# A gated delta-rule block on one core: ScalarE's copies of the turned inverse are queued behind the evictions that are counted off ahead of the level steps

## The chip, the cores and the metric

The kernel runs on one core of a Trainium2 chip. The metric is the device time of one execution in microseconds (us). The core has five engines that each work through a queue of instructions in order: PE (TensorE, matmuls), DVE (VectorE), ACT (ScalarE), POOL (GpSimd) and SP (SyncE, which here only issues DMAs). In the rows of the profile PEld is the loading of weights on PE, and L924 is line 924 of the kernel's file.

## The reference

The program is one block of a network on a sequence of 1024 tokens of width 1024: a modulated norm, dilated attention of 8 heads beside a gated delta rule of 8 heads, an output projection, and a gated feed-forward layer. What matters here is the delta rule, which works in chunks; the kernel solves the triangular system below with an explicit inverse.

```python
def _chunk_gated_delta_rule(q, k, v, g, beta):
    ...
    a_mat = jnp.where(strict, jnp.einsum('nbhcd,nbhed->nbhce', k_beta, kc) * decay, 0.0)
    rhs = jnp.concatenate([vc * bc[..., None], k_beta * jnp.exp(gcum)[..., None]], axis=-1)
    sol = lax.linalg.triangular_solve(a_mat + jnp.eye(CHUNK, dtype=a_mat.dtype), rhs,
                                      left_side=True, lower=True, unit_diagonal=True)
    u, w = sol[..., :dv], sol[..., dv:]
    ...
    _, o = lax.scan(step, state0, (qc, kc, u, w, gcum, qk))

def reference(x, c, w_ada, ...):
        ...
        proj = h @ w_in[l]
        q_a, k_a, v_a, q_d, k_d, v_d, z_d, b_d, a_d = jnp.split(proj, split_points, axis=-1)
        y_attn = _dilated_attention(q_a.reshape(hs), k_a.reshape(hs), v_a.reshape(hs), rel_bias).astype(x.dtype)
        y_delta = _gated_deltanet(q_d, k_d, v_d, z_d, b_d, a_d, conv_w[l], a_log[l], dt_bias[l], delta_norm_g[l])
        y = jnp.concatenate([y_attn, y_delta], axis=-1) @ w_out[l]
        x = x + g1 * y
        ...
```

## The kernel before

**Stages.** The eight delta heads are worked in two groups of four, `delta(0)` and `delta(1)`. Each group convolves and turns its q and k, prepares the decayed products, inverts a triangular matrix per chunk of 128 tokens, and then scans the chunks. Attention, the output projection and the feed-forward layer follow. All products in full precision are split into a high and a low part and take three matmuls each (high by high, high by low, low by high).

**Projections as filler.** The other projections of the input (`others()`: z0, kd, qd, vd, z1, va0, a4_0, a0_0, va1 and so on) are a Python generator that yields after each step with an estimate of its time. The group's code draws steps from it: `ahead(us)` draws so many microseconds, `turn(name)` draws the amount that the table `FILL` has for a product and queues that product on PE behind the last matmul drawn, and `hold(what, us)` draws until a projection is done and then so many microseconds more. A projection of kind `proj_d` (kd, qd, vd, a4, a0) makes two halves of 512 tokens, eight steps of three matmuls each (L590); one of kind `proj_t` (z, va) makes eight row blocks, eight steps of three matmuls each (L613). After a half or a block its eviction is traced, when the generator is asked for the next step: two copies of 128x256 in `spill` (L1096), one in `va_evac` (L1087) or an activation in `z_evac`. The evictions run on ScalarE under `urgent()`, which puts them early in the scheduler's preference. Sums lie in two PSUM banks ("g"), and the evicted copies in four SBUF buffers (tag "ev", bufs=4), each of which is written out to DRAM by a DMA on SP's queue (L1097, L1088).

**Order.** Each engine's queue is written ahead of the run by a scheduler that goes by priorities and by its own estimate of when an instruction's inputs are ready. `tc.issue_after(ins)` adds an order on the engine of `ins`: what is traced in its block is queued behind `ins`, without a wait for its end.

**The inverse.** `delta_inverse(g, st)` inverts 32x32 blocks on VectorE (the loop of L886 and L890 fills `tt`), writes `tt` to DRAM (L893) and loads it back in another layout as `tn` (L895). Then come the level steps, per head a generator `head(hl_)`: its first part does the product `lv` (L918) on PE from `tn`, clears `U` and a part of `t64`, turns the blocks of `tn` into `U` on VectorE (L923) and copies two blocks of `tn` into `t64`, the lower half of a tile `tc_` (L924 and L925, on ScalarE, 32x256 each). The second product fills `lv` again (L933, L937), ScalarE copies its results into `t64` and `U` (L939 to L941), and the products `lw` (L947, reads `t64`) and `lx` (L955) follow, with a copy into `U` (L957). The heads are started four steps apart (`SKEW`), but tiles `tc_` have three buffers, so three heads' copies can be done early. Ahead of the first head the kernel calls `hold(*LEVELS[g])`, which is ("qd", 4) in group 0 and ("z1", 46) in group 1, and takes `front`, the last matmul drawn; the first part of each head is queued behind it on PE. Nothing orders the ScalarE copies of that first part.

Of the kernel before, what the change touches and what calls it, by code (L numbers as in the profile page):

```python
# [12 lines left out]
AF = mybir.ActivationFunctionType  # L13
# [69 lines left out]
def build(tc, I, out):  # L83
    nc = tc.nc
# [20 lines left out]
    def urgent():  # L105
        return tc.high_priority(offset=6000)
# [40 lines left out]
    def gbank(name):  # L147
        return psb(name, "g", 2)
# [4 lines left out]
    def tbank(name):  # L153
        return psb(name, "t", 2)
# [36 lines left out]
    for j in range(3):  # L191
        n = min(HALF, 1152 - HALF * j)
        ps = tbank(f"ps_R{j}")
# [242 lines left out]
    for i in range(2):  # L436
        ps = aux[:, P * i : P * i + P]
# [119 lines left out]
        nc.scalar.activation(dst, dst, AF.Silu)  # L557

    kd, qd = {}, {}
    last = [None]  # L560
    fill = [None]
    used = [0.0]

# [11 lines left out]
    @contextmanager  # L575
    def turn(name):

        with tc.issue_after(last[0].ins) if ahead(FILL.get(name, 0)) else ExitStack():
            yield
# [43 lines left out]
    for q in range(2):  # L623
        ps = gbank(f"g_qd{q}")
# [5 lines left out]
    def z_evac(g):  # L630
        def f(tb, ps):
            zt = pv.tile([P, 256], F32, name=f"zt{g}_{tb}", tag="ev", bufs=4)
            with urgent():
                nc.scalar.activation(zt, ps[:, 0:256], AF.Silu)
            nc.gpsimd.tensor_tensor(
                out=zt.rearrange("p (h d) -> p h d", h=4),
                in0=zt.rearrange("p (h d) -> p h d", h=4),
                in1=ngh.unsqueeze(1).to_broadcast([P, 4, 64]), op=ALU.mult,
            )
            nc.sync.dma_start(_.zg[TB * g + tb], zt)  # L640
        return f
# [56 lines left out]
    def bc(v, n):  # L698
        return v.unsqueeze(len(v.shape)).to_broadcast(list(v.shape) + [n])
# [167 lines left out]
    def delta_inverse(g, st):  # L867

        nt = pr.tile([P, 32, 32], F32, name=f"nt{g}", tag="dt", bufs=2)
        nc.sync.dma_start(nt.rearrange("p j i -> p (j i)"), _.lt[g])  # L870
        bpr = pd.tile([P, 32], F32, name=f"bpr{g}", tag="nbpT", bufs=1)
        nc.sync.dma_start(
            bpr, bass.AP(tensor=_.bp[g].tensor, offset=_.bp[g][0:1, :].offset, ap=[[32, P], [1, 32]])
        )
        nc.vector.tensor_tensor(
            out=nt, in0=nt, in1=bpr.unsqueeze(1).to_broadcast([P, 32, 32]), op=ALU.mult
        )
        tt = pr.tile([P, 32, 32], F32, name=f"tt{g}", tag="dt", bufs=2)
        ttf = tt.rearrange("p i c -> p (i c)")
        nc.gpsimd.memset(ttf, 0.0)  # L880
        nc.gpsimd.memset(ttf[:, 0:1024:33], 1.0)
        for j in range(31):
            m = 31 - j
            tmp = pd.tile([P, 256], F32, name=f"tm{g}_{j}", tag="tm", bufs=1)
            tv = tmp[:, 0 : m * (j + 1)].rearrange("p (i c) -> p i c", i=m)
            nc.vector.tensor_tensor(  # L886
                out=tv, in0=bc(nt[:, j, j + 1 : 32], j + 1),
                in1=tt[:, j, 0 : j + 1].unsqueeze(1).to_broadcast([P, m, j + 1]), op=ALU.mult,
            )
            nc.vector.tensor_tensor(  # L890
                out=tt[:, j + 1 : 32, 0 : j + 1], in0=tt[:, j + 1 : 32, 0 : j + 1], in1=tv, op=ALU.add
            )
        nc.sync.dma_start(_.tn[g], ttf)  # L893
        tn = pr.tile([P, 32, 32], F32, name=f"tn{g}", tag="dt", bufs=2)
        nc.sync.dma_start(  # L895
            tn,
            bass.AP(tensor=_.tn[g].tensor, offset=_.tn[g][0:1, :].offset, ap=[[32, P], [4096, 32], [1, 32]]),
        )
        st["U"] = []

        def head(hl_):

            lt = st["lts"][hl_]
            nb = st["nbp"][:, :, hl_]
            tnh = tn[:, hl_ : 32 : 4, :]
            U = pd.tile([P, 8, P], F32, name=f"U{g}_{hl_}", tag="lu", bufs=5)
            st["U"].append(U)
            tc_ = pd.tile([P, 8, 64], F32, name=f"tc_{g}_{hl_}", tag="tc", bufs=TCB)
            t64, c2 = tc_[0:64], tc_[64:128]
            cs = pd.tile([P, 8, 32], F32, name=f"cs{g}_{hl_}", tag="cs", bufs=2)  # L910
            ps = tbank(f"lv{g}_{hl_}")
            pv = ps.rearrange("p (a n c) -> p a n c", a=2, n=8)
            with turn(f"la{g}_{hl_}"):
                for n in range(8):
                    for b in (0, 2):
                        lo = slice(32 * b, 32 * b + 32)
                        up = slice(32 * b + 32, 32 * b + 64)
                        nc.tensor.matmul(pv[up, 0, n, :], lt[lo, n, up], tnh[lo, n, :], start=True, stop=True)  # L918
            nc.gpsimd.memset(U, 0.0)
            nc.gpsimd.memset(t64[0:32, :, 32:64], 0.0)  # L920
            for b in range(4):
                bs = slice(32 * b, 32 * b + 32)
                nc.vector.transpose(U[bs, :, bs], tnh[bs])  # L923
            nc.scalar.copy(t64[0:32, :, 0:32], tnh[0:32])  # L924
            nc.scalar.copy(t64[32:64, :, 32:64], tnh[32:64])  # L925
            yield
            for b in (0, 2):
                up = slice(32 * b + 32, 32 * b + 64)
                nc.vector.tensor_tensor(out=cs[up], in0=pv[up, 0], in1=bc(nb[up], 32), op=ALU.mult)
            yield  # L930
            with turn(f"lb{g}_{hl_}"):
                for n in range(8):
                    nc.tensor.matmul(pv[32:64, 1, n, :], U[32:64, n, 32:64], cs[32:64, n, :], start=True, stop=True)  # L933
                    for b in (0, 2):
                        lo = slice(32 * b, 32 * b + 32)
                        up = slice(32 * b + 32, 32 * b + 64)
                        nc.tensor.matmul(pv[lo, 1, n, :], cs[up, n, :], U[up, n, up], start=True, stop=True)  # L937
            yield
            nc.scalar.copy(t64[32:64, :, 0:32], pv[32:64, 1])  # L939
            nc.scalar.copy(U[0:32, :, 32:64], pv[0:32, 1])  # L940
            nc.scalar.copy(U[64:96, :, 96:128], pv[64:96, 1])  # L941
            yield
            ps = sbank(f"lw{g}_{hl_}")
            pw = ps.rearrange("p (n c) -> p n c", n=8)
            with turn(f"lc{g}_{hl_}"):
                for n in range(8):
                    nc.tensor.matmul(pw[64:128, n, :], lt[0:64, n, 64:128], t64[:, n, :], start=True, stop=True)  # L947
            yield
            nc.vector.tensor_tensor(out=c2, in0=pw[64:128], in1=bc(nb[64:128], 64), op=ALU.mult)
            yield  # L950
            ps = tbank(f"lx{g}_{hl_}")
            px_ = ps.rearrange("p (n c) -> p n c", n=8)
            with turn(f"ld{g}_{hl_}"):
                for n in range(8):
                    nc.tensor.matmul(px_[0:64, n, :], c2[:, n, :], U[64:128, n, 64:128], start=True, stop=True)  # L955
            yield
            nc.scalar.copy(U[0:64, :, 64:128], px_[0:64])  # L957

        heads = []
        for step in range(3 * SKEW + 8):  # L960
            for h in heads:
                next(h, None)
            if step % SKEW == 0 and step // SKEW < 4:
                if step == 0:
                    hold(*LEVELS[g])
                    front, quiet[0] = last[0].ins, True
                heads.append(head(step // SKEW))
                with tc.issue_after(front):
                    next(heads[-1])
        quiet[0] = False  # L970
# [112 lines left out]
    def va_evac(c):  # L1083
        def f(tb, ps):
            t = pv.tile([P, 256], F32, name=f"va{c}_{tb}", tag="ev", bufs=4)
            with urgent():
                nc.scalar.copy(t, ps[:, 0:256])  # L1087
            nc.sync.dma_start(_.va[c][:, :, tb].rearrange("i p d -> p i d"), t.rearrange("p (i d) -> p i d", i=2))  # L1088
        return f

    def spill(name, dst):
        def f(hf, ps):
            for i in range(2):
                t = pv.tile([P, 256], F32, name=f"sp_{name}_{hf}_{i}", tag="ev", bufs=4)
                with urgent():
                    nc.scalar.copy(t, ps[:, 256 * i : 256 * i + 256])  # L1096
                nc.sync.dma_start(dst[:, HALF * hf + 256 * i : HALF * hf + 256 * i + 256], t)  # L1097
        return f

# [77 lines left out]
    quiet = [False]  # L1177
# [256 lines left out]
    ps = abank("g2t")  # L1434
# [82 lines left out]
    for hf in range(2):  # L1517
# [4 lines left out]
        for d in range(KT):  # L1522
            slabs = [(wsplit(I["wo"][d, 0], 512, f"wo{d}_0_{hf}"), 0)]
            t = x2[d, hf]
            nc.sync.dma_start(t, _.xp[2 * d + hf])
            ps = (gbank, sbank)[d % 2](f"wo{d}_0_{hf}")
# [204 lines left out]
    for k in range(4):  # L1731
# [3 lines left out]
        t = px.tile([P, HALF], F32, name=f"t2_{k}", tag="m", bufs=5)  # L1735
# [232 lines left out]
```

## Time and profile before

| | |
|---|---|
| time, median of 3 runs | 1410.61 us (1410.28 to 1413.69) |
| time of the profiled execution | 1409.24 us |
| its span in the profile | 1407.2 us |
| mean granted clock of TensorE | 0.993 |
| PE busy | 1347.5 us (96%) |
| ScalarE busy | 661.7 us (47%) |
| DVE busy | 875.2 us (62%) |
| tc copies from tn (L924, L925) | 16 in all, 404 ns each (median) |

The profile is of one execution, which took a little less than the median of the runs. A row of the timeline gives the start in us from the span's start, the duration, the engine, the line, the operation with its tiles and shapes, and in brackets the idle time ahead of it and what ended that. A row of waits gives who waited for whom, the total in us, the number of times and the longest. A row of the view by stages gives the busy time of each engine in a stretch of the span, with the number of instructions in brackets.

### The profile page before, as it was taken

What the parts mean: (1) busy time and instruction counts of PE and PEld (TensorE: products, weight loads), DVE (VectorE), ACT (ScalarE), POOL (GpSimd) and SP (SyncE); (2) the same over time, 40 slices, a digit from 0 to 9 for tenths busy, and PEclk for the clock granted to TensorE, in tenths of its full rate; (3) what the DMA queues carried; (4) which work ended last, traced back from release to release, by engine and by line L of the source; (5) the groups of instructions that cost most, each with busy time, mean ns of one, the idle gap of its engine ahead of it and who ended that gap; (6) DMA issues with size and microseconds to landing.
All of it is one profiled execution on the core that took longest, in us unless ns stands there. A gap on an engine that the chain in (4) does not pass through costs nothing.

```text
span 1407.2 us, 24465 instructions
## 1 busy us (share of the span) xinstructions
PE 1347.5 (96%) x8984; PEld 1109.5 (79%) x8984; DVE 875.2 (62%) x1669; ACT 661.7 (47%) x1287; POOL 285.8 (20%) x267
## 2 busy tenths in 40 slices
PE   8999999998989899999989999999999999999997
PEld 4778877888878677777877878888888888888885
DVE  3687484656815533666227986667585776474487
ACT  4497514356224355766147743333333333444456
POOL 2345412444303344453153000000000000000000
PEclk9999999999999999999999999999999999999999
DMA  8665575486352345621485345545363665765566
GB/s 307 224 194 167 153 214 164 134 255 186 109 143 65 125 138 145 195 97 61 160 247 175 130 158 171 173 148 174 131 206 105 213 211 185 253 224 194 195 225 232
DMA packets 169872, 245.68 MB, mean 175 GB/s; under 512 B 32566, under 2 KB 73831, under 8 KB 169752
## 3 DMA queue, kind: packets, MB, share of 16 engines
q1 hardware_dynamic: 169752, 244.12, 53.5%
q8 instruction: 71, 1.16, 0.3%
q14 instruction: 49, 0.40, 0.1%
HBM read 181.30 MB, written 67.48 MB: 177 GB/s over the span
## 4 chain that ended last, share of the span: by engine, by line
PE 58%; DVE 3%; DMA 2%; issue 1%; ACT 1%; POOL 0%; SPq 0%; DVEq 0%; ACTq 0%; POOLq 0%
PE wua L1590 8%; PE wga L1590 8%; PE X L1785 6%; PE wo L590 5%; PE wgc L1590 4%; PE wuc L1590 4%; PE Z L1785 4%; PE g_a L590 3%; PE y L1348 3%; PE wgb L1590 2%; PE Y L1785 2%; PE wub L1590 2%; PE tr L1331 2%; PE S L1307 1%; PE S L1308 1%
## 5 line engine op out<-in xcount | busy, mean ns | idle before, releaser
L1580 DVE TENSOR_TENSOR wl_db<-wr_db,wh_db 128x512 fp32r<-128x512 f32 x77 | 53.2, 691 | 76.2 <-ACT wh_db L1579 75.9
L1579 ACT CAST wh_db<-wr_db 128x512 fp32r<-128x512 f32 x77 | 47.9, 622 | 98.4 <-PE X L1785 41.3
L1311 DVE CUSTOM_DVE_ANT_0 X<-S,ng 128x512 f32<-128x512 f32 (+3 forms) x64 | 36.9, 586 | 56.2 <-PE S L1308 37.8
L1785 PE MATMUL X<-wl_db,wh_da 128*128 128x512 f32 x176 | 68.6, 390 | 0.2 <-DVE wl_db L1580 0.2
L1785 PE MATMUL X<-wh_db,wh_da 128*128 128x512 f32 x176 | 68.6, 390 | 0.0
L1785 PE MATMUL X<-wh_db,wl_da 128*128 128x512 f32 x176 | 68.5, 389 | 0.0
L1316 ACT ACTIVATE X<-X,sc 128x128 f32<-128x128 f32 (+7 forms) x64 | 49.4, 773 | 38.3 <-DVE sc L1311 34.8
L1318 POOL TENSOR_SCALAR X<-X,sc 128x128 f32<-128x128 f32 (+7 forms) x64 | 50.5, 792 | 75.9 <-DVE sc L1317 72.6
L1580 DVE TENSOR_TENSOR wl_da<-wr_da,wh_da 128x512 fp32r<-128x512 f32 x77 | 52.7, 685 | 1.2 <-ACT wh_da L1579 1.2
L590 PE MATMUL g_a<-hh,wh_a 128*128 128x512 f32 x128 | 52.8, 412 | 0.0
L590 PE MATMUL wo<-yh,wh_wo 128*128 128x512 f32 x128 | 51.3, 403 | 0.8 <-DVE xo L1399 0.8
L590 PE MATMUL wo<-yl,wh_wo 128*128 128x512 f32 x128 | 50.4, 393 | 1.1 <-DVE yl L1410 1.1
L590 PE MATMUL g_a<-hh,wl_a 128*128 128x512 f32 x128 | 51.2, 400 | 0.0
L590 PE MATMUL g_a<-hl,wh_a 128*128 128x512 f32 x128 | 51.1, 399 | 0.0
L590 PE MATMUL wo<-yh,wl_wo 128*128 128x512 f32 x128 | 51.0, 398 | 0.0
L1579 ACT CAST wh_da<-wr_da 128x512 fp32r<-128x512 f32 x77 | 47.3, 616 | 5.9 <-PE wua L1590 5.8
L1331 PE MATMUL tr<-ident,X 128*128 128x128 f32 x288 | 44.0, 277 | 3.6 <-DVE et L1334 2.0
L1579 ACT CAST wh_wg_s<-wg_s 128x512 fp32r<-128x512 f32 x33 | 20.6, 623 | 56.1 <-PE wuc L1590 23.8
L231 POOL TENSOR_TENSOR wl_wo<-wr_wo,wh_wo 128x512 fp32r<-128x512 f32 x24 | 32.9, 1374 | 61.6 <-ACT wh_wo L230 61.6
L613 PE MATMUL g_va<-wh_va,hh 128*128 128x256 f32 x128 | 38.6, 301 | 5.8 <-ACT sp_a L1096 5.8
L1331 PEld LDWEIGHTS tr<-ident,X 128*128 128x128 f32 x288 | 33.2, 140 | 13.3 <-issue 4.3
L1348 PE MATMUL y<-et,va 128*64 128x128 f32 x576 | 43.2, 280 | 0.3 <-DVE yl L1360 0.3
(544 smaller groups left out, 4304.3 us busy)
## 6 DMA issues: line engine op xcount, KB each, us to landing
wm<-in_wada SPq DMA_DIRECT2D x44, 512.0 KB, 6.2
wr_da<-ao_d SPq DMA_DIRECT2D x77, 256.0 KB, 3.0
wr_wu<-in_wu SPq DMA_DIRECT2D x50, 256.0 KB, 2.8
wr_wg<-in_wg SPq DMA_DIRECT2D x48, 256.0 KB, 2.8
ao_d<-a SPq DMA_DIRECT2D x44, 256.0 KB, 2.3
wr_wd<-in_wdn SPq DMA_DIRECT2D x44, 256.0 KB, 3.0
wr_db<-wt_d SPq DMA_DIRECT2D x44, 256.0 KB, 2.8
ao_d<-as SPq DMA_DIRECT2D x33, 256.0 KB, 2.0
```

The source lines that it names most:

```text
L231: (eng or nc.gpsimd).tensor_tensor(out=lo[:, :n], in0=raw[:, :n], in1=hi[:, :n].bitcast(F32), op=ALU.subtract)
L590: last[0] = nc.tensor.matmul(ps, a[:, w0], b[k0 + k4][:, cs], start=(i == 0), stop=(i == n - 1))
L613: last[0] = nc.tensor.matmul(ps[:, :n], a[k][:, ts_], b[:, w0], start=(i == 0), stop=(i == 23))
L1311: nc.vector.tensor_tensor_reduce(out=X[:, c0:c1], in0=ps[:, 0 : c1 - c0], in1=ng[:, u + c0 : u + c1], scale=1.0, scalar=(3e38 if m is None ...
L1316: nc.scalar.activation(X[:, 0:nk], X[:, 0:nk], AF.Exp, scale=-1.0, bias=m, accum_out=sc[:, 2:3])
L1318: nc.gpsimd.tensor_scalar(out=X[:, 0:nk], in0=X[:, 0:nk], scalar1=sc[:, 3:4], scalar2=0.0, op0=ALU.mult, op1=ALU.add)
L1331: nc.tensor.transpose(ps[:, (kb - c0) * P : (kb - c0 + 1) * P], X[:, kb * P : kb * P + P], ident)
L1348: nc.tensor.matmul(yps[64 * e : 64 * e + 64, yc], va[:, kb, 64 * e : 64 * e + 64], ets[e][:, kb, :], start=(kb == 0), stop=(kb == qb),)
L1579: nc.scalar.copy(hi, src)
L1580: (eng or nc.vector).tensor_tensor(out=lo, in0=src, in1=hi.bitcast(F32), op=ALU.subtract)
L1590: nc.tensor.matmul(ps, a[:, w0], b, start=(first and k == 0 and n_ == 0), stop=(k == 3 and n_ == 2), skip_group_check=True,)
L1785: nc.tensor.matmul(bank[b], a[:, ts_], w, start=(first and f == 0 and n_ == 0), stop=(f == NF - 1 and n_ == 2), skip_group_check=True,)
```

## The change

The evictions of the other projections are remembered as they are traced: `taken[0]` is the last one. At the first step of the level steps, after the hold, each group keeps that eviction as `evicted`, beside `front`. The two ScalarE copies from `tn` into `t64` of all four heads are then traced under `tc.issue_after(evicted.ins)`: they are queued on ScalarE behind that eviction, and so behind all that were traced ahead of it, since evictions follow one another. No instruction is added, removed or resized.

```diff
-    last = [None]
+    last, taken = [None], [None]
...
             zt = pv.tile([P, 256], F32, name=f"zt{g}_{tb}", tag="ev", bufs=4)
             with urgent():
-                nc.scalar.activation(zt, ps[:, 0:256], AF.Silu)
+                taken[0] = nc.scalar.activation(zt, ps[:, 0:256], AF.Silu)
...
-            nc.scalar.copy(t64[0:32, :, 0:32], tnh[0:32])
-            nc.scalar.copy(t64[32:64, :, 32:64], tnh[32:64])
+            with tc.issue_after(evicted.ins):
+                nc.scalar.copy(t64[0:32, :, 0:32], tnh[0:32])
+                nc.scalar.copy(t64[32:64, :, 32:64], tnh[32:64])
...
                 if step == 0:
                     hold(*LEVELS[g])
-                    front, quiet[0] = last[0].ins, True
+                    front, evicted, quiet[0] = last[0].ins, taken[0], True
...
             t = pv.tile([P, 256], F32, name=f"va{c}_{tb}", tag="ev", bufs=4)
             with urgent():
-                nc.scalar.copy(t, ps[:, 0:256])
+                taken[0] = nc.scalar.copy(t, ps[:, 0:256])
...
                 t = pv.tile([P, 256], F32, name=f"sp_{name}_{hf}_{i}", tag="ev", bufs=4)
                 with urgent():
-                    nc.scalar.copy(t, ps[:, 256 * i : 256 * i + 256])
+                    taken[0] = nc.scalar.copy(t, ps[:, 256 * i : 256 * i + 256])
```

## The prediction

> **What bounds the kernel now.** First the head of the page, to see which engine sets the time.
>
> ```profile
> span 1407.2 us, 24465 instructions
> PE 1347.5 (96%) x8984; PEld 1109.5 (79%) x8984; DVE 875.2 (62%) x1669; ACT 661.7 (47%) x1287; POOL 285.8 (20%) x267
> ```
>
> PE is busy 1347.5 of 1407.2 us: it is the bound, and only time in which PE stands still, or runs slowly, can be won. Next the waits, asked for around the two places where the touched copies (tc, L924 and L925) run, 200 to 222 us (group 0) and 381 to 398 us (group 1).
>
> ```profile
> PE g_vd L590 <- ACT sp_qd L1096: 0.7, 1, 0.7
> ...
> ACT tc L924 <- DMA tn<-tn_d: 8.8, 1, 8.8
> PE g_va L613 <- ACT sp_a L1096: 5.8, 1, 5.8
> ```
>
> In group 1 PE stands 5.8 us for an eviction by ScalarE (sp_a), and ScalarE stands 8.8 us in a copy for the DMA of tn. Then the timeline of both engines, to see whether one is the cause of the other.
>
> ```profile
> 386.04 0.39 PE L590 MATMUL g_a<-hh,wl_a 128*128 128x512 f32 x1
> ...
> 389.02 0.28 PE L613 MATMUL g_va<-wl_va,hh 128*128 128x256 f32 x1
> 395.06 0.58 PE L613 MATMUL g_va<-wh_va,hh 128*128 128x256 f32 x1 [5.77 <-ACT sp_a L1096]
> ```
>
> ```profile
> 393.00 0.40 ACT L924 COPY tc<-tn 32x256 f32<-32x256 f32 x1 [8.82 <-DMA tn<-tn_d]
> ...
> 393.85 0.62 ACT L230 CAST wh_a<-wr_a 128x512 fp32r<-128x512 f32 x1
> 394.37 0.64 ACT L1096 COPY sp_a<-g_a 128x256 f32<-128x256 f32 x2
> ...
> 396.57 0.37 ACT L1087 COPY va<-g_va 128x256 f32<-128x256 f32 x1
> ...
> 409.43 0.37 ACT L1087 COPY va<-g_va 128x256 f32<-128x256 f32 x1 [2.51 <-PE g_va L613]
> 412.31 0.37 ACT L1087 COPY va<-g_va 128x256 f32<-128x256 f32 x1 [2.50 <-DMA va_d<-va]
> 414.95 0.36 ACT L939 COPY tc<-lv 32x256 f32<-32x256 f32 x1 [2.27 <-PE lv L937]
> ```
>
> PE ends the sums that sp_a reads at about 386.4 us, but the eviction starts at 394.37, because the first head's two copies stand ahead of it in ScalarE's queue and wait for tn until 393.00. PE has two g banks; it fills the other one (24 matmuls to 389.14) and then stands until 395.06. Last the stretches around the stall:
>
> ```profile
> 389.40:395.00 5.60, 0.00 (x0) 0.00 (x0) 1.74 (x4) 1.96 (x6) 0.46 (x1) 0.91 0.98 230
> 395.00:400.70 5.70, 5.64 (x26) 5.64 (x27) 0.00 (x0) 1.95 (x7) 0.81 (x1) 0.50 0.61 174
> 400.70:412.00 11.30, 11.30 (x96) 11.30 (x94) 0.00 (x0) 1.43 (x4) 0.00 (x0) 1.00 0.65 182
> ```
>
> The columns are PE, PEld, DVE, ACT and POOL busy with their counts, then granted clock, DMA share and GB/s. After the stall the granted clock is 0.50: 26 matmuls take 5.64 us, where later 96 take 11.30, or 0.118 us each. At that pace 26 take 3.06 us; 2.58 us go lost behind the stall, as part of its price.
>
> **The change, part by part.** No instruction is added or removed. In each group the eight copies get an order, not a wait: behind the eviction last traced at the hold. Which that is follows from the matmuls between the hold's products and the first L918.
>
> ```profile
> L613 PE MATMUL g_va<-wh_va,hh 128*128 128x256 f32 x48 | 14.9, 311 | 5.8 <-ACT sp_a L1096 5.8
> ...
> L590 PE MATMUL g_vd<-hh,wh_vd 128*128 128x512 f32 x9 | 3.7, 414 | 0.7 <-ACT sp_qd L1096 0.7
> ```
>
> In group 1, 48 hi-by-hi matmuls are six row blocks of eight. A block's eviction is traced when the generator goes on to the next, so the hold knows five: the copies go behind the one at 409.43. In group 0 nine steps are eight of the hold and one of fill drawn afterwards, so sp_vd was not yet traced and the copies go behind the second sp_qd copy. Head 3's copies run later anyway; six copies per group move.
>
> *Removed in group 1.* The 5.77 us stall and the 2.58 us at half clock, 8.35 us, less what is late next. That is the buffer: all evictions share four "ev" buffers, filled in turn, each free when its spill has landed.
>
> ```profile
> 385.85 0.32 SPq L893 DMA_DIRECT2D tn_d<-tt  x1
> 386.26 0.38 SPq L1097 DMA_DIRECT2D qk_d<-sp_a  x1
> 388.53 0.37 SPq L895 DMA_DIRECT2D tn<-tn_d  x1
> 388.99 2.64 SPq L1097 DMA_DIRECT2D qk_d<-sp_a  x1
> ```
>
> ```profile
> tn<-tn_d SPq DMA_DIRECT2D x1, 512.0 KB, 4.5
> ...
> qk_d<-sp_a SPq DMA_DIRECT2D x1, 128.0 KB, 2.5
> ...
> DMA to landing us min/median/max: 1.7/2.6/4.6
> ```
>
> The first half of the stalled sp_a can go at 386.5. Its second half needs the buffer whose spill was issued at 386.26 and lands 2.5 us on, at 388.76; with 0.37 us of copy (the va row has the same shape) the bank is free at 389.13, just as PE comes for it at 389.14: 0 to 0.2 us, I take 0.1. Next, the eviction of the first va block needs the buffer whose spill is issued at 388.99. That issue takes 2.64 us instead of 0.38, so it is backed up behind the small packets of tn. Its landing has no row: by the median 2.6 us it would be 391.6 and nothing waits; by the longest, 4.6 us, 393.6, and the bank would be free at 393.96. PE's second block ends at about 389.2 + 24 x 0.118 = 392.0. So the new stall is 0 to 2.0 us. tn, ahead on the same queue, lands at 388.53 + 4.5 = 393.03, so I take the late side: landing 393.3, stall 1.7. Nothing later in that group is bound by buffers: blocks come 2.8 us apart.
>
> Does a stall of 1.7 us halve the clock too? Short stalls in this trace:
>
> ```profile
> 146.00:149.90 3.90, 1.85 (x25) 1.47 (x24) 2.91 (x5) 3.67 (x4) 3.44 (x2) 1.00 0.32 54
> 149.90:153.00 3.10, 3.10 (x51) 2.87 (x50) 2.16 (x3) 1.54 (x2) 1.52 (x2) 1.00 0.09 17
> ...
> 134.00:136.00 2.00, 1.13 (x9) 0.81 (x8) 1.71 (x7) 1.03 (x3) 0.74 (x1) 1.00 1.07 264
> ...
> 138.00:139.00 1.00, 1.00 (x13) 1.00 (x12) 1.00 (x2) 1.00 (x5) 1.00 (x1) 0.50 0.70 218
> ```
>
> After 2.05 us without PE work at 146 to 150 the clock stays 1.00; after 0.87 us at 134 to 136 it is 0.50 two us later. Mostly no, therefore; I count 0 and keep 2.58 for a rival. The Trainium skill ("TensorE: Matmul & The Clock Gate", Part 1) says that the clock halves after an idle window of about 3.4 us and comes back after about 3.4 us of work. By that rule the slow stretch would have cost 1.7 us and not 2.6, and the sum would be 0.9 us smaller. The trace does not agree: the row at 395 shows 5.64 us of work at 0.50, so I go by the row.
>
> *Removed in group 0.* PE's 0.7 us wait goes. Behind it:
>
> ```profile
> 212.06 0.41 ACT L924 COPY tc<-tn 32x256 f32<-32x256 f32 x1 [4.52 <-DMA tn<-tn_d]
> ...
> 216.57 0.64 ACT L1096 COPY sp_qd<-g_qd 128x256 f32<-128x256 f32 x2
> ...
> 217.25 0.67 ACT L1096 COPY sp_vd<-g_vd 128x256 f32<-128x256 f32 x2
> 220.87 0.37 ACT L939 COPY tc<-lv 32x256 f32<-32x256 f32 x1 [2.95 <-PE lv L937]
> ```
>
> ```profile
> 211.19 0.46 SPq L1097 DMA_DIRECT2D pj_d<-sp_qd  x1
> ...
> DMA to landing us min/median/max: 3.3/3.3/3.3
> ```
>
> Here too sp_qd's second half waits for a buffer: the spill at 211.19 plus 3.3 is 214.5, its copy ends at 214.9. PE comes for the bank at 217.25 - 0.7 = 216.55, so the gain is the whole 0.7 us, with 1.7 us to spare.
>
> *Moved: the six copies.* They cost 0.41 us each, 2.5 us a group, in places where ScalarE idles. Group 0: 214.9 to 217.4; queued behind them is sp_vd, up to 0.8 us late, whose bank PE needs only after the other half's 24 matmuls; L939 at 220.87 is 3.5 us away. Group 1: 409.8 to 412.3, just ahead of the next va eviction; L939 follows 2.7 us later (all of this shifts together). Who waits for the copies is the product L947 behind L939, so the move costs nothing until it slips by 2.7 us. No order is put on SP's or POOL's queue; the spills and the split of wh_a only become ready sooner.
>
> *Sum.* 5.8 + 2.58 + 0.7 - 0.1 - 1.7 = 7.3 us. PE is the bound afterwards:
>
> ```profile
> 437.00:500.00 63.00, 55.60 (x355) 47.40 (x354) 34.15 (x110) 25.01 (x67) 22.95 (x27) 1.00 0.36 113
> 500.00:600.00 100.00, 95.84 (x646) 75.43 (x645) 49.49 (x148) 59.51 (x127) 43.57 (x41) 1.00 0.52 152
> 600.00:700.00 100.00, 98.22 (x736) 77.96 (x735) 53.49 (x158) 49.57 (x109) 35.84 (x38) 1.00 0.30 103
> ```
>
> Loads there are issued as PE and its evictions progress, so they move earlier with it; I let all 7.3 us through. The profiled execution took 1409.24 us (its span and 2.04 around it): 1401.9. The median of the runs shown, 1410.61, lies 1.37 above it, so the forecast for a median is 1403.3. Its own range: no new stall gives 9.1 us (1401.5); the longest new stalls, 2.0 and 0.2 us, give 6.9 (1403.7), and with one more wait of 1.7 us, met by a PE that comes earlier, 1405.4.
>
> **The rivals.** (1) *The half clock comes back.* The new stall is followed by a slow stretch as the one at 138 was; 7.3 - 2.58 = 4.7 us are left: 1405.9. For it: 138. Against: 146 to 153.
>
> (2) *The buffers bind, and the order does little.* If the stalled sp_a takes a buffer of the pair spilled from 388.99 on, it cannot start before 393.6 at the longest landing, ends at 394.0, and PE starts at 394.1 instead of 395.06, still at half clock. Left are 1.0 + 0.7 us: 1408.9. For it: DMA share 0.98 during the stall. Against: four buffers in turn give it the older pair. The case that the change names an eviction ahead of the blocked ones and so does nothing, 1410.6, goes with this one; the counts of 48 and 9 speak against it.
>
> (3) *Slower: the order of later work comes out looser.* Queue orders are written ahead of the run from estimated times; copies taken at another moment may shift how attention's products are mixed with projections behind 437 us. Between 437 and 500 PE idles 7.4 us of 63 (12%), between 500 and 700 only 4.2 + 1.8 us. Were these 200 us as loose, idle would be 23.5 us in place of 6.0: 17.5 lost, 10.2 net, 1420.8. It decides from 7.3 us of new idle on. Against it: the copies are short, go where ScalarE idles, and no matmul's readiness in the estimate hangs on them.
>
> **How the numbers follow.** About 0.3%, 4.2 us, is what can be told from no change. Chances: forecast 0.70, rival (1) 0.10, rival (2) 0.10, rival (3) 0.10. Faster: the forecast and half of (1), whose 4.7 us lie just over the line: 0.75. Same: the other half and (2): 0.15. Slower: 0.10. The range goes from 1400.5 (9.1 us and 1 us of spread) to 1409.0, which takes in (1) and (2) and leaves out (3) and some of the tails.
>
> **What would show it.** Right: sp_a's second copy starts near 388.8 (less 0.7), six tc copies stand behind five va copies on ACT, the 5.8 us wait is gone, PE waits about 1.7 us for the first va eviction near 392, and the clock stays 1.00 up to the first L918, which comes about 7 us sooner. Wrong: a wait of over 3 us for sp_a or va, a clock of 0.50 after it, PE waiting at L947 for tc L925, or more than 7.4 us of idle in the 63 us that now begin at 437.

## The result, and the profile after

The changed kernel is a little faster: 1407.35 us (median of 11 runs, 1398.24 to 1408.76) against 1411.4 us of the kernel before on the same chip (11 runs, 1405.68 to 1415.06). The ratio is 0.9962 with a 95% interval of 0.9948 to 0.9977, which is 5.4 us won (3.2 to 7.3). A second set of runs of the same kernel, with new runs of the kernel before (median 1412.49), gave 0.9952 (0.9935 to 0.9969), or 6.8 us. The forecast was 1403.3 us (1400.5 to 1409.0) and 7.3 us won.

The head of the page of the changed kernel's profiled execution (1406.77 us) shows the same work in a span 2.5 us shorter:

```profile
span 1404.7 us, 24467 instructions
...
PE 1349.1 (96%) x8984; PEld 1110.7 (79%) x8984; DVE 876.6 (62%) x1669; ACT 662.6 (47%) x1287; POOL 287.1 (20%) x267
```

PE's timeline: the first row is the wait in group 0 that the change was also to clear; the others are, in group 1, the last g_a matmul, the matmul that now waits, and the first level product.

```profile
215.74 0.50 PE L590 MATMUL g_vd<-hh,wh_vd 128*128 128x512 f32 x1 [0.66 <-ACT sp_qd L1097]
...
389.00 0.39 PE L590 MATMUL g_a<-hh,wl_a 128*128 128x512 f32 x1
...
396.85 0.39 PE L613 MATMUL g_va<-wh_va,hh 128*128 128x256 f32 x1 [1.48 <-ACT va L1088]
...
408.55 1.20 PE L918 MATMUL lv<-tn,dt 32*32 32x32 f32 x64
```

The wait of 5.77 us for sp_a is gone; in its place PE waits 1.48 us for the first va eviction. A good local measure is the stretch from the last g_a matmul to the first L918, since it holds the same matmuls in every kernel here but e8_dummy: 386.04 to 412.16 before, 26.12 us; 389.00 to 408.55 after, 19.55 us. So 6.57 us are won at this place. The two spans differ by 2.5 us only, since the clock of PE was halved more often elsewhere in the changed kernel's execution (five places against two): that lost 8.2 us there and 3.4 us before, if each us of PE work at 0.50 is counted as half a us lost. In group 0 the 0.66 us wait for sp_qd stands as it did (0.68 before).

ScalarE's timeline in group 1, after:

```profile
389.25 0.62 ACT L230 CAST wh_a<-wr_a 128x512 fp32r<-128x512 f32 x1 [2.10 <-PE g_a L590]
389.77 0.37 ACT L1097 COPY sp_a<-g_a 128x256 f32<-128x256 f32 x1
391.81 0.37 ACT L1097 COPY sp_a<-g_a 128x256 f32<-128x256 f32 x1 [1.68 <-DMA qk_d<-sp_a]
396.43 0.65 ACT L1088 COPY va<-g_va 128x256 f32<-128x256 f32 x2 [4.24 <-DMA qk_d<-sp_a]
400.86 0.37 ACT L1088 COPY va<-g_va 128x256 f32<-128x256 f32 x1 [3.79 <-DMA qk_d<-sp_a]
...
405.82 0.37 ACT L1088 COPY va<-g_va 128x256 f32<-128x256 f32 x1 [2.51 <-PE g_va L613]
406.09 0.40 ACT L925 COPY tc<-tn 32x256 f32<-32x256 f32 x1
...
408.17 0.41 ACT L926 COPY tc<-tn 32x256 f32<-32x256 f32 x1
408.70 0.37 ACT L1088 COPY va<-g_va 128x256 f32<-128x256 f32 x1
411.34 0.36 ACT L940 COPY tc<-lv 32x256 f32<-32x256 f32 x1 [2.26 <-PE lv L938]
```

No copy from tn stands ahead of sp_a any more; six stand behind the fifth va eviction, and L940 follows 2.79 us behind the first L918, as before. What holds sp_a's second half and the first va eviction is now their buffers: both wait for a DMA that writes an earlier sp_a out. The va eviction at 400.86 waits for one as well, but PE does not wait for it. SP's timeline says why the DMA ahead of 396.43 is late:

```profile
391.49 0.37 SPq L895 DMA_DIRECT2D tn<-tn_d  x1
391.96 3.01 SPq L1098 DMA_DIRECT2D qk_d<-sp_a  x2
```

The spills issued behind the load of tn take 3.01 us to be issued, and the buffer they free is taken at 396.43. The view by stages shows that the short wait did not slow the clock (columns PE, PEld, DVE, ACT and POOL busy, granted clock, DMA share, GB/s):

```profile
394.50:396.60 2.10, 0.87 (x8) 0.66 (x6) 0.65 (x2) 0.17 (x1) 0.00 (x0) 1.00 0.80 201
396.60:402.00 5.40, 5.15 (x43) 5.15 (x44) 1.09 (x3) 0.85 (x3) 0.00 (x0) 1.00 0.79 261
...
433.30:496.30 63.00, 56.29 (x352) 48.39 (x351) 34.15 (x110) 24.66 (x65) 22.16 (x27) 0.97 0.36 110
```

After the wait 43 matmuls take 5.15 us at clock 1.00, where before 26 took 5.64 us at 0.50. The last row is the stage that began at 437 before, moved by 3.7 us (the first L918 comes 3.6 us earlier): 6.7 us of idle, 7.4 before. The queues of PE, DVE and POOL hold the same instructions in the same order in both kernels; on SP one load of weights and one spill changed places.

### The profile page after: what moved, and what is told of

Its sections match the earlier page's. It is cut to its first block, busy times and chain, and to the rows that moved or that the text cites. A ratio compares the mean times of both kernels' runs of the same rounds, so it can differ in the third digit from the quotient of the medians.

```text
span 1404.7 us, 24467 instructions
## 1 busy us (share of the span) xinstructions
PE 1349.1 (96%) x8984; PEld 1110.7 (79%) x8984; DVE 876.6 (62%) x1669; ACT 662.6 (47%) x1287; POOL 287.1 (20%) x267
## 4 chain that ended last, share of the span: by engine, by line
PE 56%; DMA 4%; DVE 3%; ACT 2%; issue 1%; POOL 1%; SPq 0%; DVEq 0%; ACTq 0%; POOLq 0%
PE wua L1591 9%; PE wga L1591 8%; PE X L1786 6%; PE wuc L1591 4%; PE wgc L1591 4%; PE Z L1786 4%; PE g_a L590 3%; PE wo L590 3%; PE y L1349 3%; PE wgb L1591 2%; PE Y L1786 2%; PE wub L1591 2%; PE tr L1332 2%; PE S L1308 1%; PE S L1309 1%
## 5 line engine op out<-in xcount | busy, mean ns | idle before, releaser
L1580 ACT CAST wh_wu_s<-wu_s 128x512 fp32r<-128x512 f32 x33 | 20.4, 621 | 43.8 <-PE wga L1591 17.2
```

The costliest lines, as they stand in the source:

```text
L1580: nc.scalar.copy(hi, src)
```

## The experiments

Each kernel ran beside the kernel before on the same chip; the ratios are to that. "Stretch" is the local measure above.

| kernel | median us (runs) | ratio, 95% interval | stretch us |
|---|---|---|---|
| e1_group1 | 1404.33 (6) | 0.9944, 0.993 to 0.9959 | 19.44 |
| e10_group1b | 1406.71 (12) | 0.9957, 0.9939 to 0.9974 | 19.68 |
| e2_group0 | 1411.2 (12) | 0.9996, 0.9983 to 1.001 | 24.93 |
| e7_after2 | 1405.87 (8) | 0.9952, 0.9935 to 0.9969 | 19.53 |
| e6_before2 | 1412.49 (10) | 0.9995, 0.9972 to 1.0018 | 25.97 |
| e4_ready | 1407.03 (8) | 0.9953, 0.9936 to 0.997 | 19.40 |
| e8_dummy | 1412.58 (10) | 0.9996, 0.9974 to 1.0019 | 23.45 |
| e3_spill_first | 1406.53 (7) | 0.9955, 0.9938 to 0.9972 | 17.59 |
| e9_both | 1404.38 (7) | 0.9947, 0.9924 to 0.997 | 17.59 |
| e5_double | 1410.0 (10) | 0.9992, 0.9963 to 1.0021 | 19.46 |

**One group at a time (e1_group1, e10_group1b, e2_group0).** The order is kept in one group only.

```diff
-            with tc.issue_after(evicted.ins):
+            with tc.issue_after(evicted.ins) if g == 1 else ExitStack():    # e1, e10; g == 0 in e2
```

> The order is put on the copies of group 1 alone. My theory: all of the gain is made in group 1, where the copies held two evictions back and PE stood 5.77 us and then ran at half clock. The stretch on PE from the last matmul ahead of the va blocks to the first L918 is 26.1 us before and about 19.6 us in the changed kernel; here it is 19.6 again, and the time is that of the changed kernel (about 5.4 us below before). Rival A (both groups give part): the time is 0.7 us or more above the changed kernel's. Rival B (the gain is chance of the clock): the stretch is short, but the time stays within 2 us of before.

> The order in group 1 alone, a second time, as the kernel to compare with on the same chip. Theory: the stretch is 19.5 us again, and the time 6 to 8 us below the kernel before (ratio 0.9943 to 0.9957). Rival (its 0.9944 was the luck of six runs): the ratio is 0.997 or more.

> The order is put on the copies of group 0 alone. My theory: nothing, because the eviction there waits for its buffer (its spill lands at about 215 us) whether the copies stand ahead of it or behind it; PE still waits 0.7 us for sp_qd, group 1's stretch on PE is 26.1 us as before, and the time is within 1 us of before but for chance. Rival A: PE's wait of 0.7 us is gone and the time is 0.7 us lower.

Group 1 alone gives the whole gain, 7.9 us in one set and 6.1 us in the other; group 0 alone gives nothing that can be told. PE's waits in e2_group0 from 381 to 400 us show the old stall in full:

```profile
PE g_va L613 <- ACT sp_a L1097: 5.4, 1, 5.4
```

Its stretch is 1.2 us shorter than before all the same, by a slightly shorter stall and less half clock behind it. PE's wait for sp_qd in group 0, expected at 0.7 us, was 1.88 us in this execution.

**Only the wait taken away (e4_ready).** The copies stay where the planner puts them, but read another tile that is ready.

```diff
-            nc.scalar.copy(t64[0:32, :, 0:32], tnh[0:32])
-            nc.scalar.copy(t64[32:64, :, 32:64], tnh[32:64])
+            nc.scalar.copy(t64[0:32, :, 0:32], lt[0:32, :, 0:32])
+            nc.scalar.copy(t64[32:64, :, 32:64], lt[32:64, :, 32:64])
```

> The kernel before, but the two copies read the diagonal blocks of lt, which is there early, instead of tn; so t64 lacks the inverse's diagonal blocks. The copies are as many and as long as before, and nothing is ordered behind an eviction. Theory (what costs is the wait for tn at the head of ScalarE's queue): the copies run early, PE's 5.8 us wait for sp_a is gone, the stretch on PE from the last g_a matmul to the first L918 falls from 26.1 to about 19.5 us as with the change, and the time is 5 to 8 us below the kernel before. Rival (the 2.5 us of copying on ScalarE, or the transfer of tn itself, holds the eviction): the stretch stays above 23 us and the time within 3 us of the kernel before.

The stretch is 19.40 us and the gain 6.6 us (4.2 to 9.0), as with the change. The PE timeline has the same new wait as the changed kernel:

```profile
396.53 0.39 PE L613 MATMUL g_va<-wh_va,hh 128*128 128x256 f32 x1 [1.49 <-ACT va L1087]
```

So the price was the wait for tn at the head of ScalarE's queue, not the copying, and tn's transfer alone costs PE 1.5 us and not 5.8.

**PE kept busy in the stall (e8_dummy).** The kernel before, with 48 matmuls that nothing needs ahead of the second va block.

```diff
+            if (name, tb) == ("va1", 1):
+                wh, wl = slabs[0]
+                dummy = sbank("dummy")
+                for i in range(48):
+                    last[0] = nc.tensor.matmul(
+                        dummy[:, :n], hh[0][:, 0:P], wh[:, 0:n], start=(i == 0), stop=(i == 47)
+                    )
```

> The kernel before, with 48 matmuls of 128x256 into an unused bank between the first and second row block of va1, about 5.7 us of work that no result needs; PE is busy where it stood still for sp_a. Theory (the half clock behind the stall follows from the stall): the eviction of sp_a still starts at about 394, the clock behind it is 1.00, and the stretch from the last g_a matmul to the first L918 falls from 26.1 by about 2.6 to 23.5 us, half clock at other places aside. Rival (the half clock at 395 came by chance or from the heavy transfers, not from the stall): 0.50 for some us behind the dummies as before, and the stretch stays at 26 us.

PE's timeline and the view by stages:

```profile
393.36 5.92 PE L610 MATMUL dummy<-wh_va,hh 128*128 128x256 f32 x48
399.12 0.39 PE L620 MATMUL g_va<-wh_va,hh 128*128 128x256 f32 x1
```

```profile
393.00:399.00 6.00, 6.00 (x52) 6.00 (x51) 1.75 (x4) 1.91 (x6) 0.40 (x1) 1.00 0.89 209
399.00:405.00 6.00, 6.00 (x52) 5.96 (x51) 0.00 (x0) 2.31 (x7) 0.88 (x1) 1.00 0.63 170
```

The useful work begins again 5.76 us behind the dummies' start, 8.86 us behind the last g_a matmul (9.02 before), but at full clock: the stretch is 23.45 us, 2.67 less than before. Of that 0.16 is the earlier start and 2.51 the matmuls at full clock, where the prediction had put the slow ones at 2.58. The half clock at this place is thus a cost of the stall. The time of the whole does not show it (0.9996), since its interval is 6 us wide.

**The buffers freed sooner (e3_spill_first, e9_both).** In e3_spill_first the changed kernel's hold in group 1 comes ahead of the write of `tt`, which is queued behind the spill of a0's first half; so the spills do not stand behind tn. e9_both has that and the order of the copies in group 1 alone.

```diff
-        nc.sync.dma_start(_.tn[g], ttf)
+        if g == 1:
+            hold(*LEVELS[g])
+        with tc.issue_after(spilled["a0_0", 0].ins) if g == 1 else ExitStack():
+            nc.sync.dma_start(_.tn[g], ttf)
...
-                    hold(*LEVELS[g])
+                    if g == 0:
+                        hold(*LEVELS[g])
```

> The changed kernel, and in group 1 the write of tt (L893) is queued on SP behind the spills of a0_0's first half, so that these no longer stand behind a wait for tt. My theory: the 1.5 us that PE still waits for the first va eviction is a wait for an ev buffer whose spill is issued late; here sp_a's second copy and the first va eviction start as soon as PE is done, that wait is gone and the stretch on PE is 18.0 to 18.2 us in place of 19.6; the time is 1.5 us below the changed kernel's. Rival (the small packets of tn or ScalarE itself hold the evictions): the wait stays within 0.5 us of 1.5 us. A second rival: tn comes later by the loads now ahead of it and the first L918 waits for it, which gives back up to 2 us.

> The order in group 1 alone, with the spill of a0's first half ahead of the small-packet transfers tn_d and tn as well. Theory (both waits in group 1 are real, each on PE's path): PE waits neither for sp_a nor for va there, the stretch from the last g_a matmul to the first L918 is about 17.6 us against 26.1 before and 19.5 with the order alone, so the time is 8 to 9 us below the kernel before (ratio 0.9937 to 0.9945), 2 us below the order alone. Rival (what the second edit wins is given back, because tn then starts 3 us later and the heads wait for it): the stretch is 17.6 us but PE has a new wait behind the first L918, and the time equals that of the order alone or is above it.

ScalarE's timeline in e9_both, in which line 1102 is the copy of spill and 1093 that of va:

```profile
388.04 0.64 ACT L1102 COPY sp_a<-g_a 128x256 f32<-128x256 f32 x2
390.62 0.37 ACT L1093 COPY va<-g_va 128x256 f32<-128x256 f32 x1 [1.94 <-issue]
393.50 0.37 ACT L1093 COPY va<-g_va 128x256 f32<-128x256 f32 x1 [2.51 <-PE g_va L614]
```

and PE's stage up to the first L918 (404.86) in the view by stages:

```profile
387.00:404.80 17.80, 17.80 (x147) 17.61 (x146) 1.74 (x4) 5.26 (x14) 1.30 (x1) 1.00 0.91 216
```

Both halves of sp_a go at once and each va copy follows its block; PE has no idle time at all, at full clock, and the stretch is 17.59 us in both kernels, 1.96 us less than with the change. A new wait behind the first L918 did not appear: from there to the first product `lx` it is 5.55 us, as in the changed kernel. In time e3_spill_first missed what was expected, 1.5 us below the changed kernel: its median is 0.7 us above that of e7_after2 on the same chip. The median of e9_both is the lowest beside e1_group1's, but its ratio (7.5 us won, 4.2 to 10.7) cannot be told from that of the order alone on the same chip (6.1 us, 3.7 to 8.6). That the second edit gains 2 us of time is seen in the trace and not in the times.

**The copies doubled (e5_double).** Each ordered copy of the changed kernel is done twice.

```diff
+                for _i in range(2):
                     nc.scalar.copy(t64[0:32, :, 0:32], tnh[0:32])
+                for _i in range(2):
                     nc.scalar.copy(t64[32:64, :, 32:64], tnh[32:64])
```

> The changed kernel, with each of the ordered copies done twice, so 6 x 0.41 = 2.5 us more on ScalarE per group ahead of L940. Theory (copies behind the evictions lie in 2.7 to 3.5 us of slack): group 1's first L940 comes at most about 0.5 us later behind the first L918 than in the changed kernel, group 0's not at all, and the time is within 1.5 us of the changed kernel, -4 to -7 us against the kernel before. Rival (the moved copies already sit on the path): every copy counts, 2.5 us per group, 5 us in all, and the time comes back to within 1.5 us of the kernel before.

In group 1, ScalarE's timeline (L942 is the copy that was L940):

```profile
408.24 0.37 ACT L1090 COPY va<-g_va 128x256 f32<-128x256 f32 x1 [2.51 <-PE g_va L613]
408.51 0.40 ACT L926 COPY tc<-tn 32x256 f32<-32x256 f32 x1
...
412.87 0.84 ACT L928 COPY tc<-tn 32x256 f32<-32x256 f32 x2
413.75 0.36 ACT L942 COPY tc<-lv 32x256 f32<-32x256 f32 x1
```

The twelve copies just fit: L942 starts 2.79 us behind the first L918 (410.96), the same as in the changed kernel, so the slack there is real and the single copies cost nothing. In group 0 it starts 4.75 us behind, against 2.74. Most of that is half clock at 218 to 224 us: e1_group1, which has no order in group 0, fell into half clock at the same place and shows 4.06. At most about 0.7 us is left for the copies, so "not at all" was wrong there. The time by the ratio is 1.1 us below the kernel before, where the rival had put it, but the interval (5.2 below to 3.0 above) reaches into the theory's range, and the ten runs spread from 1405.58 to 1423.19 us; it decides nothing between them. Its profiled execution fell into half clock at eight places, the changed kernel's at five. Whether the added copies have a part in that is not shown.

**The two kernels again (e7_after2, e6_before2).** Both are unaltered.

> The changed kernel once more, unaltered. My theory: the stretch on PE in group 1 is 19.6 us again within 0.3 us, and PE's wait for the first va eviction is 1.5 us again; what differs from the other execution are the places where the granted clock is 0.50 (five stretches there, three in the profile of before). Rival (the change itself loosens the work between the two groups): the time from the first L939 of group 0 to the end of group 1's inverse is again 4 us longer than before the change, in this execution too.

> The kernel before, unaltered, for a second trace of it. Theory (half clock comes at places that differ from one execution to the next, in pieces of about 3.4 us of PE time): the wait of 5.8 us for sp_a and the slow matmuls behind it are there again, and the other stretches at 0.50 lie at other places than 116 and 138 us, between 2 and 8 of them. Rival (they belong to fixed places in the code): 0.50 at 116, 138 and 395 us and nowhere else, and the execution takes 1409 us within 1 us.

The stretch repeats to 0.15 us in both (19.53 and 25.97). The rival of e7_after2 falls: from the first copy from `lv` in group 0 (L939, L940 in the changed kernel) to the write of `tt` in group 1 (L893) it is 165.0 us in the trace of before and 169.4 in the changed kernel's, but 168.0 in e6_before2 and 167.1 in e7_after2. What differs from execution to execution is the half clock elsewhere. In e6_before2 four stretches lie outside the stall, within the count of its theory; three are at new places, but one, at 135 to 142 us, covers 138 again. At 343.6 us PE waits in both traces of the kernel before for the same activation, equally long, once with and once without half clock behind it. From the trace of before, timeline and stages:

```profile
343.64 0.55 PE L857 MATMUL trv<-ident,vd 128*128 128x128 f32 x3 [2.36 <-ACT vd L557]
```

```profile
344.00:350.00 6.00, 6.00 (x53) 6.00 (x52) 5.14 (x5) 1.41 (x2) 0.00 (x0) 1.00 0.78 224
```

and from that of e6_before2:

```profile
343.60 0.66 PE L857 MATMUL trv<-ident,vd 128*128 128x128 f32 x2 [2.38 <-ACT vd L557]
```

```profile
344.00:350.00 6.00, 6.00 (x41) 6.00 (x40) 4.51 (x5) 1.44 (x2) 0.00 (x0) 0.74 0.65 176
```

53 matmuls against 41 in the same 6 us.

## Why the prediction was right, and where it was not

**The stall and its half clock (5.8 and 2.58 us): right in size and cause.** e4_ready shows that the wait for tn was the cause, e8_dummy prices the half clock at 2.51 us, and e9_both, where nothing new takes the stall's place, has a stretch 8.53 us shorter than before, for 8.35 in the sum.

**The new buffer waits (0.1 and 1.7 us): right.** Their sum is the 1.96 us between the stretches of the changed kernel and of e9_both. The prediction's sp_a copy near 388.8 and the va eviction late at 393.3 are, moved by the 2.96 us by which this execution reached the place later, 391.8 and 396.3; the rows say 391.81 and 396.43. The choice of the late side for the landing, because tn stands ahead in the queue, was what made this term right. "Nothing later in that group is bound by buffers" does not hold for ScalarE (the row at 400.86), but PE had no use for that bank yet. Group 1 therefore came out at 6.57 us, for 6.55 in the sum.

**The 0.7 us in group 0: wrong, it is zero.** The step that failed is the landing of the spill, taken as 3.3 us. The view that it was read from has minimum, median and maximum alike because it holds one landing only, that of the spill issued at 192.93, some 10 us ahead of the transfers of tn. ScalarE's timeline of the changed kernel, and SP's:

```profile
212.12 0.36 ACT L1097 COPY sp_qd<-g_qd 128x256 f32<-128x256 f32 x1
215.32 0.37 ACT L1097 COPY sp_qd<-g_qd 128x256 f32<-128x256 f32 x1 [2.83 <-DMA pj_d<-sp_qd]
```

```profile
204.88 0.37 SPq L895 DMA_DIRECT2D tn<-tn_d  x1
205.34 4.56 SPq L1120 DMA_DIRECT2D wm<-in_wada  x2
209.95 1.47 SPq L1098 DMA_DIRECT2D pj_d<-sp_qd  x3
```

The copy no longer waits for tn, but the buffer comes free only at 215.32, 5.4 us behind the first of those issues, which stand behind tn and two loads of 512 KB (which of them delays it is not shown); PE's wait is as before. This wait also swings by itself: it is 0.2 to 2.4 us in the five traces with the order in group 0, and 0.5 to 1.8 us in the seven without it. The largest of the seven is e4_ready's, where no copy waits for tn at all. In group 1 the same kind of wait had been given the late side; here a landing from a quieter place was taken and "1.7 us to spare" was read off it.

**The rest of the miss.** The forecast lies 4.05 us below the measured median: 0.8 us are the kernel before itself, 1411.4 in that comparison for 1410.61 in the runs shown, 0.7 are the group 0 term, and the other 2.55 lie inside the spread of a comparison whose interval is 4 us wide. The local gain of 6.57 us lies within the interval of the first set (3.2 to 7.3) and of the second (4.4 to 9.2). That all of it passes through to the end agrees with both; the times can't show it closer than that. The traces add an estimate: the span less the stretch less what half clock elsewhere lost is 1377.9 us on average in the three traces with the long stall (1376.2 to 1379.9) and 1378.1 in the five with the short wait and single copies (1376.9 to 1379.8). So what the stretch wins is not given back later, as far as a spread of 4 us lets one see; the four kernels with other edits, 1370.7 to 1375.2, are left out.

**The rivals.** (1) Half clock after the new wait: not seen in the changed kernel, whose clock stays 1.00 up to the first L918, nor behind the same wait (1.36 to 1.61 us) in five other traces. The prediction's reason, two short stalls elsewhere, was thin, and the last section shows that such a wait is not safe in general. (2) Buffers bind: they do, but at 1.5 us on PE and one buffer later than this rival had it; and the change names the eviction that was counted out, the fifth of six. (3) A looser later order: fell, as PE's queue order did not change at all and the 63 us of the next stage hold no more idle than before.

## What to carry to other kernels

An engine that is 47% busy can still stall the engine that is the bound, if an instruction waiting for a DMA stands ahead of an eviction in its queue; price that by its wait and by the slow clock behind it. When the waiting instruction is moved away, ask which buffer the freed eviction needs, and take its landing late where the write-out stands behind a transfer of many small packets or behind large loads (4.5 and 5.4 us here from the issue to the eviction that used the buffer, against landings of 2.5 and 3.3 us in quieter places). A local stretch with the same matmuls in every kernel settled here in one trace what the times of whole executions could not.

## What the runs showed of the hardware

Half clock came in stretches at places that changed from one execution to the next, with PE's order unchanged. In the records of the granted clock in the twelve traces, which begin at 16 to 19 us, every such stretch up to the end of PE's work lasts 3.41, 6.83 or 10.24 us, and within one execution all starts and ends lie a whole multiple of 3.41 us apart, to 0.002 us. So the clock is set for one window of 3.41 us at a time, on a grid that lies elsewhere in each execution, and a window full of work at 0.50 costs about 1.7 us. The profiled executions had from two stretches (e1_group1, 1404.41 us) to eight (e5_double, 1414.56 us, and e3_spill_first, 1410.56 us).

The grid explains why the waits of 2.36 and 2.38 us at one place were followed by half clock in one execution and not in the other. In e6_before2 one window holds the whole wait (views by stages, cut at the grid):

```profile
340.26:343.67 3.41, 1.03 (x8) 0.83 (x9) 0.85 (x1) 2.34 (x2) 0.00 (x0) 1.00 0.74 217
343.67:347.08 3.41, 3.41 (x17) 3.41 (x18) 1.66 (x3) 1.44 (x2) 0.00 (x0) 0.50 0.79 234
```

In the trace of before the edge of a window cuts the wait in two:

```profile
339.34:342.75 3.41, 1.94 (x39) 1.53 (x31) 1.78 (x2) 1.50 (x2) 0.60 (x2) 1.00 0.59 136
342.75:346.17 3.42, 2.53 (x22) 2.54 (x23) 1.46 (x3) 2.19 (x3) 0.00 (x0) 1.00 1.06 333
```

PE is busy for 1.03 us of the one window, and the next is at 0.50; it is busy for 1.94 and 2.53 us of the two, and the clock stays. Of all windows at full clock in the twelve traces, from 20 us on, the 21 with PE busy for up to 43.3% were all followed by half clock, of the 4351 with 85% or more none was, and of the 360 between 33 were; what decides there is not shown. The stall of 5.77 us leaves PE at most 0.53 us of work in one of its windows wherever the grid lies (an estimate: 3.41 less half of the stall), so its half clock was no chance. The new wait leaves 53% to 68% in the six traces that have it; of the 97 windows in that range at other places 15 were followed by half clock. That it was not followed here may be luck.

Behind the stall the slow stretch is two windows in all three traces that have it with PE idle. It begins while PE still stands, and the work in it is 5.7 us in the trace of before, 5.5 in e6_before2 and 3.8 in e2_group0:

```profile
390.54:393.95 3.41, 0.00 (x0) 0.00 (x0) 0.86 (x2) 0.91 (x3) 0.00 (x0) 1.00 0.92 198
393.95:397.37 3.42, 2.31 (x11) 2.31 (x12) 0.88 (x3) 2.93 (x8) 1.27 (x1) 0.50 0.51 182
397.37:400.78 3.41, 3.41 (x18) 3.41 (x18) 0.00 (x0) 0.15 (x1) 0.00 (x0) 0.50 0.86 244
```

The Trainium skill ("TensorE: Matmul & The Clock Gate", Part 1) says that the clock is judged in a window of about 3.4 us that runs freely, so that a transition depends on where in the window the work falls. The stretches of 3.41 us and their grid agree with it. So does the slow stretch at 395, which the prediction held against the page: its first window is only partly filled with work, its second is full, and then the clock is back.

Two spills of 128 KB issued right behind the transfer of tn, 512 KB, held SP's queue for 3.0 us in the changed kernel. In e9_both it is 4.1 us for the two that stand there, as SP's timeline shows, at no cost to PE:

```profile
390.45 0.38 SPq L899 DMA_DIRECT2D tn<-tn_d  x1
391.02 4.07 SPq L1094 DMA_DIRECT2D va_d<-va  x2
```
